# Key norm per token instead of per element: sums of ten columns, spread back by transposes

## The chip, the cores and the metric

The kernel runs on one core of a Trainium2 chip. The metric is device time in microseconds for one execution; the time before is 3225.3 us, the median of three runs from 3222.83 to 3228.34 us.

## What is computed

One layer of a hybrid network over 640 tokens (512 latent, 128 context). Of the input projection's columns, k (1024 wide, 16 heads of 64) goes through the part that the change touches:

```python
kk = heads(k * lp['k_k'])
kk = kk * lax.rsqrt(jnp.maximum(jnp.sum(kk * kk, axis=-1, keepdims=True), 1e-24))
...
kd = heads(k * (1.0 + (a - 1.0) * lp['k_a']))
y, s_fin = _delta_scan(rh, decay, kd, vh, -kk, kk * heads(a), ...)
# in a step: sa = S @ a_t;  S = S * w_t + outer(sa, b_t) + outer(v_t, k_t)
```

The scan meets the normalised key twice, as `a_t = -kk` (it reads the state) and as `b_t = kk * a` (it writes to it), and only as their product. Both norms may therefore stand in `b_t` alone, as one factor 1/sum.

## The kernel before

The work has three stretches. The first, up to about 1090 us, is the input projection: 43 blocks of 128 output columns, each block 16 slices of 128 inputs by two halves of 320 tokens. Every slice takes three `big` products on PE (L190 to L192; high times high, high times low, low times high). The weights come in by DMA as `raw`, ACT rounds them to `hi` (L168) and DVE subtracts to get `lo` (L169); three buffers of each turn over. The second stretch runs the recurrence chunk by chunk beside the output projection, the third is the feed-forward part.

Between the projection's products stands the preparation of the scan. The 16 heads are handled as 8 pairs, one pair on 128 partitions (channels) by 640 tokens. For each pair `take_r`, `take_v` and `take_k` are generators: they run a few instructions, then `yield` a number. A `Mixer` calls them after every second product slice with a budget; a float is charged to the budget, an integer n means "hold for n more slices". The `solve` and `merge` generators of other mixers, and the loads of modulation weights (`pm<-wt,cT`, L903), are laid between as well. The Tile framework's scheduler then sets the final order on every engine.

The key norm is in `take_k`. Before: `nkk` = k times `k_k` on DVE (L565); its square `sqk` on ACT (L567); two PE products with `bones`, a block matrix of ones, give each channel its head's sum, spread over all 64 channels of the head (`pmm`, L519, 128x320 each); DVE clamps them from PSUM into `ssq` (L570), ACT takes the root (L572), DVE inverts it (L576) and multiplies it into `nkk` with a minus sign (L578). What follows for each of two scan directions d: the low-rank products `pwa` (L592, L593), `tanh` (L596), a running sum, `exp`, the read rows `R` (L615 to L621, from `nkk`), the write rows `X` (L632, L636, from `tha` times `nkk`), then PE products of `X` and `R` (`pG`, L651), transposes `pXT` (L669) and `pW` (L683). `pmm` and `pwa` use two PSUM banks, `g0` and `g1` of pool `pk`, one buffer each; `pvt`, `pblk` and the like share two buffers `pt`. At its end `take_k` sums `fs` with `bones` into the same `g0`/`g1` banks, and DVE reads them in `zv` (L698).

Of the kernel before, what the change touches and what calls it, by code (L numbers as in the profile page):

```python
# [10 lines left out]
F32 = mybir.dt.float32  # L11
F32R = mybir.dt.float32r
BF16 = mybir.dt.bfloat16
AF = mybir.ActivationFunctionType
ALU = mybir.AluOpType
# [4 lines left out]
P = 128  # L20
D = 2048
KB = D // P
T = 640
NT = T // P
HALF = T // 2
CH = 64
# [21 lines left out]
NW = 8  # L48
# [27 lines left out]
C_KK = 140  # L76
# [13 lines left out]
def flow_step(ctx: ExitStack, tc, x_prompt, x_sample, state_rwkv, c, c_ctx, w_mod, b_mod,  # L90
# [4 lines left out]
    V, S, G, TE = nc.vector, nc.scalar, nc.gpsimd, nc.tensor  # L95
# [19 lines left out]
    ident = cp.tile([P, P], F32, name="ident")  # L115
    make_identity(nc, ident)
    I2 = cb.tile([P, CH], F32, name="I2")
    for h in range(2):
        s = slice(CH * h, CH * h + CH)
# [7 lines left out]
                         op0=ALU.mult, op1=ALU.add)  # L127
    V.tensor_sub(mask[:, 0:CH], mask[:, CH:P], I2)
    bones = cb.tile([P, P], F32, name="bones")
# [9 lines left out]
    prm = cp.tile([P, NPRM], F32, name="prm")  # L139
# [66 lines left out]
    with ExitStack() as ph:  # L206
# [92 lines left out]
        for t in range(NT):  # L299
            xt = xall[:, t, :]  # L300
            ss = p0b.tile([P, 1], F32, name="ss")
# [5 lines left out]
            for q in range(4):  # L307
                pt = ps0.tile([P, 4, P], F32, tag="pt", name="ptx")
# [31 lines left out]
        for j in range(4):  # L340
# [5 lines left out]
            for kb in range(4 * j, 4 * j + 4):  # L346
                hf = p0b.tile([P, T], F32, name="hf")
# [14 lines left out]
    bk, bp, gs, bz = (hp.enter_context(tc.tile_pool(name=n, bufs=1)) for n in ("bk", "bp", "gs", "bz"))  # L362
# [27 lines left out]

    w0h = bk.tile([P, 32], F32, name="w0h", bufs=1)
    V.tensor_scalar_mul(w0h, prm[:, C_W0:C_W0 + 32], 0.5)
    kah = bk.tile([P, 8], F32, name="kah", bufs=1)
    V.tensor_scalar_mul(kah, prm[:, C_KA:C_KA + 8], 0.5)
    ka1 = bk.tile([P, 8], F32, name="ka1", bufs=1)
# [105 lines left out]
    def both(name):  # L501
        return [pk.tile([P, 512], F32, tag=f"g{h}", name=name) for h in range(2)]
# [10 lines left out]
    def pmm(rhs_list, evac):  # L513
        two = both("pmm")
        for hf in range(2):
            s = slice(HALF * hf, HALF * hf + HALF)
            ps = two[hf][:, 0:HALF]
            for i, (l, r) in enumerate(rhs_list):
                TE.matmul(ps, l, r[:, s], start=(i == 0), stop=(i == len(rhs_list) - 1))  # L519
            evac(ps, s)  # L520
# [29 lines left out]
    def take_k(pr, p):  # L550
# [3 lines left out]
        zk = bk.tile([P, T], F32, tag="zk", name="zk")  # L554
# [7 lines left out]
        S.copy(wh, wl)  # L562
        V.tensor_sub(wr, wl, wh.bitcast(F32))
        nkk = bk.tile([P, T], F32, tag="nkk", name="nkk", bufs=1)
        V.tensor_scalar_mul(nkk, zk, prm[:, C_KK + p:C_KK + p + 1])  # L565
        sq = bk.tile([P, T], F32, tag="t1", name="sqk", bufs=2)
        S.activation(sq, nkk, AF.Square)  # L567
        yield 0.5
        ssq = bp.tile([P, T], F32, tag="t2", name="ssq", bufs=1)
        pmm([(bones, sq)], lambda ps, s: V.tensor_scalar_max(ssq[:, s], ps, 1e-24))  # L570
        yield 1.0
        S.activation(ssq, ssq, AF.Sqrt)  # L572
        yield 0.5
        for hf in range(2):
            s = slice(HALF * hf, HALF * hf + HALF)
            V.reciprocal(ssq[:, s], ssq[:, s])  # L576
            yield 2.0
        V.scalar_tensor_tensor(out=nkk, in0=nkk, scalar=-1.0, in1=ssq, op0=ALU.mult, op1=ALU.mult)  # L578
        fs = bk.tile([P, T], F32, tag="fs", name="fs", bufs=1)
        yield 0.8  # L580
        for d in range(2):
# [4 lines left out]
            tha = bp.tile([P, T], F32, tag="t3", name="tha", bufs=1)  # L586
            for hf in range(2):
                s = slice(HALF * hf, HALF * hf + HALF)
                pwa = both("pwa")
                two = [pwa[h][:, 0:HALF] for h in range(2)]  # L590
# [10 lines left out]
            for lo in (0, HALF):  # L601
                s = slice(lo, lo + HALF)
# [26 lines left out]
            V.tensor_scalar(f, tha, kah[:, p:p + 1], ka1[:, p:p + 1], op0=ALU.mult, op1=ALU.add)  # L629
            V.tensor_mul(f, f, zk)  # L630
            yield 1.2
            V.scalar_tensor_tensor(out=tha, in0=tha, scalar=1.0, in1=nkk, op0=ALU.add, op1=ALU.mult)  # L632
            yield 0.8

            for e in ((0, 1), (1, 0)):
                V.scalar_tensor_tensor(out=rev(X[hsl(e[0]), :, e[1], :]), in0=v3(tha)[hsl(e[0])], scalar=-0.5,  # L636
                                       in1=i3[hsl(e[0])], op0=ALU.mult, op1=ALU.mult)
# [11 lines left out]
            for (c0, c1) in ((0, 4), (4, 8), (8, NCH)):  # L649
                two = [ps.rearrange("p (c t) -> p c t", t=P) for ps in both("pG")]  # L650
# [5 lines left out]
                for h in (1, 0):  # L656
                    s, q, ps = hsl(h), osl(h), two[h]
# [9 lines left out]
            for (c0, c1) in ((0, 8), (8, NCH)):  # L667
                two = [ps.rearrange("p (c t) -> p c t", t=CH) for ps in both("pXT")]
# [3 lines left out]
                for h in range(2):  # L672
                    ps = two[h]
# [4 lines left out]
            two = [ps.rearrange("p (c t) -> p c t", t=CH) for ps in both("pW0")]  # L678
            for c0 in (0, 5):
                ps = two[c0 // 5][:, 0:5, :]  # L680
# [8 lines left out]
            for gq in range(8):  # L689
# [6 lines left out]
                               op0=ALU.mult, op1=ALU.mult)  # L696
# [232 lines left out]
    for p in range(NPAIR):  # L929
        block(P * p, take_r, 2.6, p)  # L930
        block(2 * DA + P * p, take_v, 5.1, p)
        block(DA + P * p, take_k, KCOST, p)
        while g < GORD[p]:
            block(CSH + DA + P * g, take_gv, 12.0, g)
            block(CSH + P * g, take_gu, 5.0, g)
            g += 1
# [36 lines left out]
    pt_ = pbx.enter_context(tc.tile_pool(name="pt_", bufs=2, space=PSUM))  # L973
# [384 lines left out]
    t1, t2 = slice(0, HALF), slice(HALF, T)  # L1358
# [67 lines left out]
    with ExitStack() as ph:  # L1426
        pss = ph.enter_context(tc.tile_pool(name="pss", bufs=1, space=PSUM))
# [5 lines left out]
                        in1=prm[:, C_N2:C_N2 + KB].unsqueeze(2).to_broadcast([P, KB, 2]), op=ALU.mult)  # L1433
        ss = [pss.tile([P, HALF], F32, name=f"ss{hf}") for hf in range(2)]
# [32 lines left out]
        def four_blocks(hf, m, q):  # L1467

            s = slice(HALF * hf, HALF * hf + HALF)
            if q == 0:  # L1470
                pool = pb2 if m % 2 or hf == 0 and m == 4 else pbig
                banks[m] = pool.tile([P, HALF], F32, tag="big", name="big")
            ps = banks[m]
            hi, lo = split(w_out[0, 4 * q * P:(4 * q + 4) * P, m * P:(m + 1) * P], 4,
                           *((wraw, wo) if q or hf or m >= AHEAD else ()))
            for k in range(4):
                kb = 4 * q + k
                TE.matmul(ps, hi[:, k, :], o_hi[kb][:, s], start=(kb == 0), stop=False)  # L1478
                TE.matmul(ps, hi[:, k, :], o_lo[kb][:, s], start=False, stop=False)  # L1479
                TE.matmul(ps, lo[:, k, :], o_hi[kb][:, s], start=False, stop=(kb == 7))  # L1480
            return ps
# [3 lines left out]
        for hf in range(2):  # L1485
            s = slice(HALF * hf, HALF * hf + HALF)
            for m in range(KB):
                if hf or m >= AHEAD:
                    four_blocks(hf, m, 0)
                ps = four_blocks(hf, m, 1)  # L1490
# [591 lines left out]
    for t in (3, 4, 0, 1, 2):  # L2082
        for h in (1, 0):
            out = fin.tile([P, 4, 256], F32, tag=f"out{h}", name="out")
# [3 lines left out]
            else:  # L2088
                V.scalar_tensor_tensor(out=out, in0=src, scalar=rse[:, t:t + 1],
                                       in1=fg[:, 4 * h:4 * h + 4], op0=ALU.mult, op1=ALU.mult)  # L2090
# [31 lines left out]
```

## Time and profile before

| | |
|---|---|
| median of 3 runs | 3225.3 us |
| profiled execution | 3226.49 us |
| its span, first to last instruction | 3224.7 us |
| PE / DVE / ACT / POOL busy over the span | 96% / 72% / 45% / 38% |
| mean granted TensorE clock | 0.990 |

The profile names groups by line, engine and operation, then output tiles `<-` input tiles. A row of a group ends with its busy time, the mean duration of one in ns, and the idle time of the engine just before it with what ended that idle time. `PEld` is the weight load. PE durations are modelled and overlap, so the distance from one start to the next tells the cost of a PE instruction better than its duration.

### The profile page before, as it was taken

To read this page: it belongs to the slowest core of one execution; us is meant where nothing else is said; L and a number is where in the kernel's file an instruction comes from. 1 tells how busy PE (TensorE), PEld (TensorE's weight loads), DVE (VectorE), ACT (ScalarE), POOL (GpSimd) and SP (SyncE) were. 2 spreads that over 40 slices of the span, in tenths; PEclk is the share of its full clock that TensorE was granted. 3 is DMA by queue.
4 is the path that set the end of the run, shared out by engine and by line. 5 is a ranking of instruction groups with operands and counts; after the bars stand their busy time and mean duration, and the time that the engine had idled before them with its cause. 6 is when DMAs were issued, how large, how long until landed. Compare 5 with 4: busy or idle time off the path is not lost.

```text
span 3224.7 us, 72310 instructions
## 1 busy us (share of the span) xinstructions
PE 3097.7 (96%) x28216; PEld 2861.5 (89%) x28216; DVE 2337.3 (72%) x4107; ACT 1460.7 (45%) x3197; POOL 1215.7 (38%) x1065
## 2 busy tenths in 40 slices
PE   6999999999999999999999999999999999999997
PEld 4688778777878888899999999999999999999997
DVE  4547666676666677767877777778788688777778
ACT  3334444444444444346644444444444454444365
POOL 2001121211122023311366556656655645555542
PEclk9999999999999999999999999999999999999999
DMA  9667786777778688564534433343344364553453
GB/s 372 220 197 203 194 215 187 204 205 197 201 197 220 193 273 268 178 197 128 149 112 125 121 117 118 117 128 120 107 130 128 104 197 151 157 157 111 145 167 121
DMA packets 740438, 550.88 MB, mean 171 GB/s; under 512 B 141056, under 2 KB 673504, under 8 KB 731264
## 3 DMA queue, kind: packets, MB, share of 16 engines
q1 hardware_dynamic: 727136, 532.47, 55.5%
q0 software_dynamic: 10624, 13.23, 1.7%
q8 instruction: 222, 3.64, 0.5%
q14 instruction: 120, 0.98, 0.1%
q10 hardware_dynamic: 2336, 0.57, 0.1%
HBM read 437.79 MB, written 110.95 MB: 170 GB/s over the span
## 4 chain that ended last, share of the span: by engine, by line
PE 72%; DVE 10%; DMA 8%; issue 5%; ACT 3%; POOL 2%; SPq 0%; DVEq 0%; POOLq 0%; ACTq 0%
PE P L1640 15%; PE P L1638 15%; PE P L1639 15%; PE big L190 5%; PE big L192 4%; PE big L191 4%; DVE lo L1420 2%; DMA wt<-in_w_mod_dram 2%; PE pm L903 1%; PE pG L651 1%; DMA raw<-in_w_in_dram 1%; PE big L1035 1%; PE big L1479 1%; PE big L1478 1%; PE big L1480 1%
## 5 line engine op out<-in xcount | busy, mean ns | idle before, releaser
L1640 PE MATMUL P<-xo,lo 128*128 128x320 f32 x2352 | 727.9, 310 | 2.2 <-DVE lo L1420 2.1
L1638 PE MATMUL P<-xo,hi 128*128 128x320 f32 x2352 | 727.5, 309 | 0.7 <-ACT hi L1419 0.7
L1639 PE MATMUL P<-xo,hi 128*128 128x320 f32 x2352 | 727.4, 309 | 0.0
L1420 DVE TENSOR_TENSOR lo<-raw,hi 128x512 fp32r<-128x512 f32 x526 | 512.0, 977 | 164.8 <-ACT hi L1419 160.3
L1419 ACT CAST hi<-raw 128x512 fp32r<-128x512 f32 x526 | 327.7, 623 | 487.6 <-PE P L1639 393.5
L190 PE MATMUL big<-h_hi,hi 128*128 128x320 f32 x1376 | 450.4, 327 | 10.1 <-ACT hi L168 6.7
L1640 PEld LDWEIGHTS P<-xo,lo 128*128 128x128 f32 x2352 | 442.1, 188 | 3.2 <-DVE lo L1420 2.9
L1638 PEld LDWEIGHTS P<-xo,hi 128*128 128x128 f32 x2352 | 442.0, 188 | 1.0 <-ACT hi L1419 1.0
L1639 PEld LDWEIGHTS P<-xo,hi 128*128 128x128 f32 x2352 | 442.0, 188 | 0.0
L192 PE MATMUL big<-h_hi,lo 128*128 128x320 f32 x1376 | 433.8, 316 | 0.8 <-DVE lo L169 0.6
L191 PE MATMUL big<-h_lo,hi 128*128 128x320 f32 x1376 | 431.7, 314 | 0.5 <-DVE h_lo L352 0.5
L1548 POOL TENSOR_TENSOR raw<-raw 128x512 f32<-128x512 f32 x252 | 406.6, 1623 | 16.4 <-DVE lo L1420 4.9
L1640 PE MATMUL P<-xd,lo 128*128 128x320 f32 x1232 | 384.9, 312 | 16.3 <-DVE lo L1420 16.3
L1638 PE MATMUL P<-xd,hi 128*128 128x320 f32 x1232 | 383.4, 311 | 1.8 <-ACT hi L1419 1.1
L1639 PE MATMUL P<-xd,hi 128*128 128x320 f32 x1232 | 382.1, 310 | 0.0
L190 PEld LDWEIGHTS big<-h_hi,hi 128*128 128x128 f32 x1376 | 261.9, 190 | 79.0 <-issue 47.8
L169 DVE TENSOR_TENSOR lo<-raw,hi 128x512 fp32r<-128x512 f32 x268 | 183.3, 687 | 195.0 <-ACT hi L168 177.7
L1419 ACT CAST hi<-rawd 128x512 fp32r<-128x512 f32 (+1 forms) x288 | 168.7, 589 | 241.9 <-PE P L1639 201.7
L192 PEld LDWEIGHTS big<-h_hi,lo 128*128 128x128 f32 x1376 | 261.3, 190 | 9.5 <-issue 2.8
L191 PEld LDWEIGHTS big<-h_lo,hi 128*128 128x128 f32 x1376 | 261.8, 190 | 6.0 <-DVE h_lo L352 1.2
L168 ACT CAST hi<-raw 128x512 fp32r<-128x512 f32 x268 | 164.9, 619 | 223.8 <-PE big L191 115.8
L1640 PEld LDWEIGHTS P<-xd,lo 128*128 128x128 f32 x1232 | 232.4, 189 | 22.9 <-DVE lo L1420 22.7
(404 smaller groups left out, 6046.4 us busy)
## 6 DMA issues: line engine op xcount, KB each, us to landing
wt<-in_w_mod_dram SPq DMA_DIRECT2D x96, 1024.0 KB
raw<-in_w_ffn_gate_dram SPq DMA_DIRECT2D x182, 256.0 KB
raw<-in_w_ffn_up_dram SPq DMA_DIRECT2D x182, 256.0 KB
rec<-d_S SPq DMA_DIRECT2D x80, 576.0 KB
raw<-in_w_in_dram SPq DMA_DIRECT2D x172, 256.0 KB
rawd<-in_w_ffn_down_dram SPq DMA_DIRECT2D x128, 256.0 KB
raw<-in_w_out_dram SPq DMA_DIRECT2D x96, 256.0 KB
xd<-d_os SPq DMA_DIRECT2D x66, 320.0 KB
```

The costliest lines, as they stand in the source:

```text
L168: S.copy(hi, raw)
L169: V.tensor_sub(lo, raw, hi.bitcast(F32))
L190: TE.matmul(halves[hf], hi[:, k, :], h_hi[:, kb, s], start=(kb == 0), stop=False)
L191: TE.matmul(halves[hf], hi[:, k, :], h_lo[:, kb, s], start=False, stop=False)
L192: TE.matmul(halves[hf], lo[:, k, :], h_hi[:, kb, s], start=False, stop=(kb == KB - 1))
L651: in_turn([lambda cc=cc, h=h: TE.matmul(two[h][:, cc - c0, :], X[hsl(h), cc].rearrange("p s t -> p (s t)"), R[hsl(h), cc].rearrange("p s t ...
L1419: S.copy(hi[:, 0:nk], raw[:, 0:nk])
L1420: V.tensor_sub(lo[:, 0:nk], raw[:, 0:nk], hi[:, 0:nk].bitcast(F32))
L1548: G.tensor_tensor(out=o[:, 0:nk], in0=p[:, 0:nk], in1=q[:, 0:nk], op=ALU.subtract)
L1638: TE.matmul(ps, hi[:, k, :], xk[:, 0, :], start=f, stop=False)
L1639: TE.matmul(ps, hi[:, k, :], xk[:, 1, :], start=False, stop=False)
L1640: TE.matmul(ps, lo[:, k, :], xk[:, 0, :], start=False, stop=l)
```

## The change

The norm is worked out with tokens on the partitions. `nkk` = minus k times `k_k` is made on ACT, with a column `nkc` prepared once. Five PE products take a 128x128 block of `sqk` as the stationary operand and two columns of `bones` as the moving one, so a token's two head sums lie in two columns (`pss`, 10 columns for 640 tokens, in a `pt` buffer). DVE clamps and inverts these ten columns (`ssk`); ACT repeats each value 64 times (`rnb`, 128x640); after a hold of `NW` = 8 slices five PE transposes put it back to channels by tokens (`pnk`, in `g0`/`g1`), and DVE multiplies it from PSUM with `nkk` into a new tile `nks`. There is no square root: the factor is 1/sum. `R` takes the plain `nkk`; only `tha`, and so `X`, takes `nks`.

```diff
+    nkc = bk.tile([P, 8], F32, name="nkc", bufs=1)
+    V.tensor_scalar_mul(nkc, prm[:, C_KK:C_KK + 8], -1.0)
...
         nkk = bk.tile([P, T], F32, tag="nkk", name="nkk", bufs=1)
-        V.tensor_scalar_mul(nkk, zk, prm[:, C_KK + p:C_KK + p + 1])
+        S.activation(nkk, zk, AF.Copy, scale=nkc[:, p:p + 1])
         sq = bk.tile([P, T], F32, tag="t1", name="sqk", bufs=2)
         S.activation(sq, nkk, AF.Square)
+        yield 0.8
+        ps = pt_.tile([P, 4, P], F32, tag="pt", name="pss")[:, 0, 0:2 * NT].rearrange("p (t h) -> p t h", h=2)
+        for t in range(NT):
+            TE.matmul(ps[:, t, :], sq[:, t * P:(t + 1) * P], bones[:, 0:P:CH], start=True, stop=True)
+        ss = bp.tile([P, NT, 2], F32, name="ssk")
+        V.tensor_scalar_max(ss, ps, 1e-24)
+        V.reciprocal(ss, ss)
+        rb = bk.tile([P, NT, 2, CH], F32, tag="t1", name="rnb", bufs=2)
+        S.copy(rb, ss.unsqueeze(3).to_broadcast([P, NT, 2, CH]))
+        yield NW
+        two = both("pnk")
+        for t in range(NT):
+            TE.transpose(two[t // 3][:, (t % 3) * P:(t % 3 + 1) * P], rb[:, t].rearrange("p h k -> p (h k)"), ident)
         yield 0.5
-        ssq = bp.tile([P, T], F32, tag="t2", name="ssq", bufs=1)
-        pmm([(bones, sq)], lambda ps, s: V.tensor_scalar_max(ssq[:, s], ps, 1e-24))
-        yield 1.0
-        S.activation(ssq, ssq, AF.Sqrt)
-        yield 0.5
-        for hf in range(2):
-            s = slice(HALF * hf, HALF * hf + HALF)
-            V.reciprocal(ssq[:, s], ssq[:, s])
-            yield 2.0
-        V.scalar_tensor_tensor(out=nkk, in0=nkk, scalar=-1.0, in1=ssq, op0=ALU.mult, op1=ALU.mult)
+        nks = bk.tile([P, T], F32, tag="nks", name="nks", bufs=1)
+        for t0, t1 in ((0, 3), (3, NT)):
+            V.tensor_mul(nks[:, t0 * P:t1 * P], nkk[:, t0 * P:t1 * P], two[t0 // 3][:, 0:(t1 - t0) * P])
...
-            V.scalar_tensor_tensor(out=tha, in0=tha, scalar=1.0, in1=nkk, op0=ALU.add, op1=ALU.mult)
+            V.scalar_tensor_tensor(out=tha, in0=tha, scalar=1.0, in1=nks, op0=ALU.add, op1=ALU.mult)
```

The new lines move the scheduler's order within the projection stretch only; on PE the last 14891 instructions stand as before. Three places follow.

On PE, at the third pair's norm, before:

```order
L192 MATMUL big<-h_hi,lo 128x320
L519 MATMUL pmm<-sqk,bones 128x320 x2
L190 MATMUL big<-h_hi,hi 128x320
L191 MATMUL big<-h_lo,hi 128x320
L192 MATMUL big<-h_hi,lo 128x320
```

and at the same pair now (`pm_3491` is a modulation product that happens to stand there):

```order
L573 MATMUL pss<-bones,sqk 128x2 x5
L191 MATMUL big<-h_lo,hi 128x320
L192 MATMUL big<-h_hi,lo 128x320
L190 MATMUL big<-h_hi,hi 128x320
L191 MATMUL big<-h_lo,hi 128x320
L192 MATMUL big<-h_hi,lo 128x320
L911 MATMUL pm_3491<-wt,cT 2x512
L582 MATMUL pnk<-ident,rnb 128x128 x5
```

Two products have become ten instructions in two groups, with five `big` products between them. In the eight pairs 9, 24, 5, 24, 9, 24, 24 and 12 `big` products stand between the groups.

On ACT, at the second pair's norm, before:

```order
L567 ACTIVATE sqk<-nkk 128x640
L168 CAST hi<-raw 128x512
L572 ACT_TABLE_LOAD
L572 ACTIVATE ssq<-ssq 128x640
L168 CAST hi<-raw 128x512
L596 ACT_TABLE_LOAD
L596 ACTIVATE sg<-pwa,w0h 128x320
```

and now:

```order
L567 ACTIVATE nkk<-zk,nkc 128x640
L569 ACTIVATE sqk<-nkk 128x640
L627 COPY R<-nkk 128x10
L168 CAST hi<-raw 128x512
L578 COPY rnb<-ssk 128x640
L168 CAST hi<-raw 128x512
L604 ACTIVATE sg<-pwa,w0h 128x320
```

Both table loads are gone (in the whole program 19 became 3), and the spread `rnb` stands behind a weight cast. That is so in pairs 2, 4, 6, 7 and 8.

On DVE, at the second pair's norm, before:

```order
L565 TENSOR_SCALAR nkk<-zk,prm 128x640
L169 TENSOR_TENSOR lo<-raw,hi 128x512
L570 TENSOR_SCALAR ssq<-pmm 128x320 x2
L576 RECIPROCAL ssq<-ssq 128x320 x2
L169 TENSOR_TENSOR lo<-raw,hi 128x512
L578 SCALAR_TENSOR_TENSOR nkk<-nkk,ssq 128x640
```

and now:

```order
L575 TENSOR_SCALAR ssk<-pss 128x10
L576 RECIPROCAL ssk<-ssk 128x10
L169 TENSOR_TENSOR lo<-raw,hi 128x512
L586 TENSOR_TENSOR nks<-nkk,pnk 128x384
L586 TENSOR_TENSOR nks<-nkk,pnk 128x256
L169 TENSOR_TENSOR lo<-raw,hi 128x512
```

The wide clamp and inversion have become narrow; the multiplication now stands in DVE's queue until PE's transposes are done.

## The prediction

> **What bounds the kernel now.** First the page's head and its table of busy times, then the busy times cut into the projection stretch that holds the whole change (139 to 1090 us), then that stretch's groups and PE's waits, then the timeline for the price of single pieces.
>
> ```profile
> span 3224.7 us, 72310 instructions
> PE 3097.7 (96%) x28216; PEld 2861.5 (89%) x28216; DVE 2337.3 (72%) x4107; ACT 1460.7 (45%) x3197; POOL 1215.7 (38%) x1065
> ```
>
> The columns of the next row are the stretch and its length, then PE, PEld, DVE, ACT and POOL with their instructions, granted clock, DMA share and GB/s.
>
> ```profile
> 139.00:1090.00 951.00, 911.38 (x10787) 768.94 (x10788) 625.82 (x1243) 436.53 (x940) 159.59 (x259) 0.99 0.72 196
> ```
>
> PE is busy 911.4 of 951 us, DVE 625.8 (66%), ACT 436.5 (46%). So PE sets the end of the stretch; all that it waits for comes to 951 - 911.4 = 39.6 us. Work taken from DVE or ACT pays only through these waits. The next rows are PE's waits there: total us, times, longest.
>
> ```profile
> PE pG L651 <- DVE X L636: 5.1, 8, 1.6
> PE pm L903 <- DMA wt<-in_w_mod_dram: 4.6, 5, 2.4
> PE pG L651 <- DVE GA L661: 3.5, 4, 2.1
> PE big L190 <- ACT hi L168: 3.2, 5, 1.0
> PE pXT L669 <- DVE GA L661: 2.8, 6, 0.7
> PE pmm L519 <- DVE zv L698: 2.8, 3, 2.0
> PE pXT L669 <- ACT XT L675: 2.7, 5, 0.7
> PE pG L651 <- DVE X L640: 1.5, 2, 1.1
> ```
>
> No row is large. One belongs to the norm itself: `pmm`, which waits for the PSUM banks that DVE still reads in `zv`.
>
> **Off PE.** The groups of the norm (count, busy us, mean ns, idle time ahead):
>
> ```profile
> L576 DVE RECIPROCAL ssq<-ssq 128x320 f32<-128x320 f32 x16 | 33.7, 2132 | 4.0 <-ACT ssq L572 4.0
> L660 DVE TENSOR_TENSOR GR<-pG,mask 128x256 f32<-128x256 f32 x64 | 27.0, 422 | 20.1 <-PE pG L651 10.0 <-DMA d_S<-GR 8.9
> L572 ACT ACT_TABLE_LOAD x8 | 10.3, 1283 | 0.1
> L596 ACT ACT_TABLE_LOAD x8 | 10.3, 1283 | 0.1
> L698 DVE TENSOR_TENSOR zv<-pmm,zv 128x320 f32<-128x320 f32 x16 | 7.7, 481 | 0.3 <-PE pmm L519 0.3
> L570 DVE TENSOR_SCALAR ssq<-pmm 128x320 f32<-128x320 f32 x16 | 7.3, 485 | 2.3 <-PE pmm L519 2.1
> L578 DVE SCALAR_TENSOR_TENSOR nkk<-nkk,ssq 128x640 f32<-128x640 f32 x8 | 6.5, 814 | 0.0
> L572 ACT ACTIVATE ssq<-ssq 128x640 f32<-128x640 f32 x8 | 5.9, 740 | 11.5 <-DVE ssq L570 11.5
> L565 DVE TENSOR_SCALAR nkk<-zk,prm 128x640 f32<-128x640 f32 x8 | 4.6, 572 | 0.1
> L747 DVE TENSOR_SCALAR gva<-gva 128x5 f32<-128x5 f32 x7 | 1.2, 172 | 0.1
> ```
>
> DVE loses per pair 0.57 + 2 x 0.485 + 2 x 2.13 + 0.81 = 6.6 us. It gains a clamp and an inversion of ten columns, about 0.2 us each (estimate: the 128x5 row's 172 ns; ten columns of the inversion at 2132/320 = 6.7 ns are 67 ns more at most), and the product out of PSUM, 384 and 256 columns: 256 cost 422 ns and 320 cost 481 ns in the rows, so 0.55 + 0.42 = 0.97 us. Net -5.2 us a pair, -42 us in all. ACT loses 2 x 1.283 + 0.74 = 3.3 us a pair and gains `nkk` and `rnb`, each about the 0.74 us of another 128x640 row; net -1.8, or -14 us in all. Together that is 56 of 1062 us, or 5%.
>
> **On PE.** Now the timeline (start, us, engine, line): the norm's two products, a group of four transposes, and a group of `pW` products on 64x64 blocks.
>
> ```profile
> 193.72 0.30 PE L192 MATMUL big<-h_hi,lo 128*128 128x320 f32 x1
> 193.93 1.34 PE L519 MATMUL pmm<-sqk,bones 128*128 128x320 f32 x4
> 194.87 0.55 PE L190 MATMUL big<-h_hi,hi 128*128 128x320 f32 x1
> 195.25 0.31 PE L191 MATMUL big<-h_lo,hi 128*128 128x320 f32 x1
> 195.40 0.31 PE L192 MATMUL big<-h_hi,lo 128*128 128x320 f32 x1
> ...
> 182.32 0.31 PE L192 MATMUL big<-h_hi,lo 128*128 128x320 f32 x1
> 182.46 0.60 PE L544 MATMUL pvt<-ident,zv 128*128 128x128 f32 x4
> 182.82 0.39 PE L190 MATMUL big<-h_hi,hi 128*128 128x320 f32 x1
> 183.05 0.31 PE L191 MATMUL big<-h_lo,hi 128*128 128x320 f32 x1
> ...
> 588.17 0.31 PE L191 MATMUL big<-h_lo,hi 128*128 128x320 f32 x1
> 588.41 0.80 PE L683 MATMUL pW<-Z,GA 64*64 64x64 f32 x20
> 589.14 0.42 PE L192 MATMUL big<-h_hi,lo 128*128 128x320 f32 x1
> 589.39 0.31 PE L190 MATMUL big<-h_hi,hi 128*128 128x320 f32 x1
> ```
>
> `big` products follow each other at 0.147 us (195.25 to 195.40). From 193.72 to 195.25 go 1.53 us; less two spacings of 0.147 that is 1.24 us for the old products. Four transposes: 182.32 to 183.05 less the same is 0.44 us, 0.11 each, so the five new ones cost 0.55 us. Twenty `pW` records: 588.17 to 589.39 less two spacings is 0.93 us, 0.046 each.
>
> The five `pss` products have no row like them: a full 128x128 f32 stationary operand and only two moving columns. An f32 product makes two records here (16 `pmm` products of the norm, 32 records), so there are ten. The lower bound is the `pW` row, 0.046 each, 0.46 us; the upper is the 0.11 us of a transpose, which loads the same weights and streams 128 columns, 1.1 us. I take 0.1 us, near the upper row, because it has the same weights. Then the new PE work is 1.0 + 0.55 = 1.55 us against 1.24: +0.31 a pair, **+2.5 us** for eight; by the bounds (0.46 and 1.1) -1.8 to +3.3 us.
>
> The Trainium skill has two rules for this piece, and they part. "TensorE: Matmul & The Clock Gate", section "Back-to-back issue gap", gives up to 64 moving columns a floor of about 25 ns, which would make ten records 0.25 us and this term -3.5 us. Its section "LDWEIGHTS (loading the stationary operand)" prices a load by its columns, P/1.2 ns, 107 ns for 128, whatever streams through, which makes it 1.07 us and this term +3.0 us: that speaks against making the wide operand the stationary one. No row here separates load and stream.
>
> The order takes switches away. A `pW` group, on part of the array, has 588.17 to 588.41 = 0.24 us ahead of it and 589.14 to 589.39 = 0.25 us behind its first `big`, where 0.147 is normal: 0.2 us a switch. Counting over the stretch's whole order, switches from `big` to groups on part of the array fall by 15 (`pXT` 40 to 29, `pG`, `pT` and `pM` by 8 together; `pblk` and `pm` rise by 4): **-3.0 us**, bounds 0 and -3.
>
> **Waits.** `pss` no longer needs the banks that `zv` holds: the `pmm` row goes, **-2.8 us**. If `pnk` meets `zv` in its place it stays; the hold makes that unlikely.
>
> The new wait is `pnk` for `rnb`: clamp 0.2, inversion 0.2 to 0.24, copy 0.74, about 1.2 us after the last `pss`. On PE 9, 24, 5, 24, 9, 24, 24 and 12 `big` products stand between, 1.3, 3.5, 0.7, 3.5, 1.3, 3.5, 3.5 and 1.8 us. Only the third pair falls short, by 0.5 us at most. But ACT and DVE work in order, and a cast stands ahead of `rnb` in five pairs; I take **+1.0 us** in all, bounds 0 and the slow rival below.
>
> The rest is the looser DVE. `X` waits behind the inversions in the first of two directions: half of 5.1 + 1.5, -3.3 us. The other waits on DVE and ACT, some 20 us of the 39.6, shrink by perhaps a tenth where the load shrinks by 5%: -2.0 us. Together **-5.3 us**; bounds 0 and -20 (half of all that PE waits).
>
> Sum: 2.5 - 3.0 - 2.8 + 1.0 - 5.3 = **-7.6 us**. The profiled execution, 3226.49 us (span 3224.7 and 1.8 around it), goes to 3218.9; it lies 1.2 us over the median, so by the median 3225.3 - 7.6 = 3217.7, forecast **3218**. Its own range is 3212 to 3222.
>
> **Rivals.** *The norm's DVE block was what the pair waited for.* The reciprocal holds DVE for 4.3 us a pair, and everything behind it, masks, `X` and `lo`, is late at once. Then half of PE's waits go in place of the 5.3: -20 and the PE terms -2.3, 3203. For it: five of the eight rows above are waits on DVE. Against it: those five are 15.7 us together, half of it on masks and `zv`, which do not follow the norm.
>
> *Nothing changes.* If DMA paces the stretch (0.72 busy, and PE waits 4.6 us for `wt`), what PE saves it waits for elsewhere: 3225. Against it: 4.6 us is all that is seen.
>
> *Slower: the transposes wait for ACT.*
>
> ```profile
> L168 ACT CAST hi<-raw 128x512 fp32r<-128x512 f32 x161 | 99.0, 619 | 129.1 <-PE big L191 112.2 <-DMA raw<-in_w_in_dram 14.4 <-issue 1.8
> ...
> ACT hi L168 <- PE big L191: 112.2, 71, 4.5
> ```
>
> A cast waits for PE to leave a weight buffer, 1.6 us on average when it waits, 4.5 at the longest. If it stands ahead of `rnb` and is released by a `big` shortly before the transposes, PE then waits for cast and copy, 0.62 + 0.74 = 1.36 us, and DVE holds its `lo` behind `nks`. It decides from a wait of 3.5 - 1.2 = 2.3 us on. In eight pairs that is +10.9; with the 5.3 lost and the other terms (2.5 - 3.0 - 2.8) it makes +7.6: 3233. For it: a cast is there in five of eight pairs. Against it: 2.3 us is above the mean.
>
> **How the numbers follow.** Forecast 0.55, large gain 0.18, nothing 0.12, slower 0.15. The range takes the large gain's centre and goes up to near the slow one, 3203 to 3230. A measurement tells about 0.2%, 6.5 us, from no change, so faster is below 3218.8. A little over half of the forecast lies there and all of the large gain: 0.3 + 0.18 = 0.48. Slower is 0.15, with 0.01 from the rest; within 0.2% is what is left, 0.36.
>
> **What would show it.** In the profile after, the stretch should have DVE near 584 us and ACT near 422; ten `pss` records about 0.1 us apart; no `pmm<-sqk` wait; rows `pnk <- ACT rnb` of at most 1 us or so in total; `X` and `GA` waits down by a third. `pss` at 0.05 apart gives 4 us more. Rows of `pnk` waiting in most pairs, with `hi` ahead of `rnb` late, would make the prediction wrong upwards; PE waits of 20 us in place of 39.6, downwards.

## The result and the profile after

| | before | after |
|---|---|---|
| median, runs | 3226.82 us (3222.83 to 3235.99, 4 runs) | 3258.62 us (3250.72 to 3262.37, 4 runs) |
| ratio | | 1.0094, 95% interval 1.0078 to 1.0110 |
| profiled execution, span | 3226.49, 3224.7 us | 3255.12, 3253.3 us |
| mean granted clock | 0.990 | 0.987 |

The change makes the kernel slower by 0.94%, about 30 us; 7.6 us less was predicted. These are the page's span and busy times after, and then the projection stretch, which now ends near 1114 us instead of 1089 (columns as in the prediction).

```profile
span 3253.3 us, 72457 instructions
PE 3115.5 (96%) x28304; PEld 2873.6 (88%) x28304; DVE 2292.9 (70%) x4092; ACT 1445.8 (44%) x3189; POOL 1219.0 (37%) x1065
```

```profile
139.00:1114.00 975.00, 927.36 (x10862) 781.99 (x10861) 584.84 (x1224) 421.95 (x927) 158.52 (x259) 0.98 0.70 191
```

Read DVE and ACT first. DVE has 584.8 us in the stretch and ACT 421.9, where 584 and 422 were forecast: what was taken off these engines is gone. But PE now needs 975 us for the stretch instead of 951. It is busy 927.4 instead of 911.4, and it stands still for 975 - 927.4 = 47.6 us instead of 39.6. The rest of the program takes 3 us more; 25 of the 29 us of span are in this stretch.

PE's waits in the stretch (total us, times, longest):

```profile
PE pm L911 <- DMA wt<-in_w_mod_dram: 7.7, 9, 1.5
PE big L190 <- ACT hi L168: 4.9, 6, 1.3
PE pG L659 <- DVE X L644: 4.2, 5, 1.7
PE pblk L851 <- issue: 3.7, 2, 3.0
PE pblk L851 <- DMA TB<-d: 3.7, 4, 1.9
PE ptm L176 <- issue: 3.0, 2, 2.6
PE pG L659 <- DVE GA L669: 2.8, 7, 0.7
PE pmm L521 <- ACT Z L693: 2.5, 3, 2.0
PE pG L659 <- DVE X L648: 2.3, 3, 1.1
```

No row is large, as before, but they are other rows. The wait for `zv` is gone. In its place stand waits of `pblk` and `ptm` (10.4 us in three rows, each of which stood at 0.7 us or less), and more for `wt`, `hi` and `Z` (2.5 us; before 0.9). The two `X` rows are 6.5 us, and a third of 1.0 us is new; before they were 6.6. `pnk` for `rnb` is not among them at all. Added up by what ended them, PE's waits on DVE and ACT fell from 33.1 to 29.0 us, and 2.8 of that is the row for `zv`. The waits on a DMA, or with no releaser named, rose from 6.5 to 18.5 us.

Now the new PE work itself, in PE's timeline of the first pair (start, us, line):

```profile
192.91 0.30 PE L190 MATMUL big<-h_hi,hi 128*128 128x320 f32 x1
193.22 1.28 PE L573 MATMUL pss<-bones,sqk 128*128 128x2 f32 x10
194.35 0.39 PE L191 MATMUL big<-h_lo,hi 128*128 128x320 f32 x1
194.58 0.31 PE L192 MATMUL big<-h_hi,lo 128*128 128x320 f32 x1
...
195.61 0.31 PE L190 MATMUL big<-h_hi,hi 128*128 128x320 f32 x1
195.76 0.77 PE L582 MATMUL pnk<-ident,rnb 128*128 128x128 f32 x5
196.29 0.39 PE L191 MATMUL big<-h_lo,hi 128*128 128x320 f32 x1
196.52 0.31 PE L192 MATMUL big<-h_hi,lo 128*128 128x320 f32 x1
```

The ten records take 193.22 to 194.35 = 1.13 us, 0.113 each, though each streams two columns. Summed from start to start over all eight pairs, `pss` is 8.9 us and `pnk` 4.9 where the two old products were 8.8: +5.0 us.

Last, what a wait costs here. The timeline of PE around one of the new waits, and then four stretches of 3.4 us around it (PE's busy time is the first number after the length, the granted clock the third from the end):

```profile
753.27 0.50 PE L851 MATMUL pblk<-TB,M 32*32 32x32 f32 x35
756.76 0.32 PE L851 MATMUL pblk<-TB,M 32*32 32x32 f32 x15 [2.99 <-issue]
757.01 1.01 PE L911 MATMUL pm<-wt,cT 128*2 128x512 f32 x4
```

```profile
750.20:753.60 3.40, 3.40 (x150) 3.17 (x137) 0.06 (x1) 0.76 (x2) 0.00 (x0) 1.00 1.05 307
753.60:757.00 3.40, 0.41 (x31) 0.28 (x20) 3.02 (x7) 1.19 (x3) 0.00 (x0) 1.00 0.21 62
757.00:760.40 3.40, 3.40 (x58) 1.64 (x48) 0.91 (x2) 0.08 (x1) 0.00 (x0) 0.51 0.28 46
760.40:763.80 3.40, 3.40 (x33) 2.81 (x33) 0.18 (x1) 1.03 (x3) 0.00 (x0) 0.98 0.83 286
```

PE waits 3 us in the second stretch and is given half the clock in the third, with work at hand: 3.4 us at 0.5 lose another 1.7. The trace's clock record has 13.6 us of half clock in this stretch of the program before and 34 us after, which is 10.2 us of clock lost on top. So the 25 us come apart as +5.0 of new PE work, +8.0 of standing still and +10.2 of half clock; some 2 us are left that I did not trace further.

Not every half-clock stretch follows a wait. One of 6.8 us begins at 610.1 us. In the 3.4 us ahead of it PE was busy throughout, but 1.03 us of that went to the ten `pss` records of the fifth pair, and 0.9 to products on 32x32 blocks:

```profile
606.70:610.10 3.40, 3.40 (x61) 2.97 (x60) 1.79 (x9) 0.92 (x2) 0.37 (x1) 1.00 0.91 263
610.10:613.50 3.40, 3.40 (x48) 2.96 (x49) 1.08 (x4) 1.08 (x4) 0.00 (x0) 0.53 1.00 304
```

### The profile page after: what moved, and what is told of

It reads as the page before. It is cut to its first block, busy times and chain, and to the rows that moved or that the text cites. A ratio compares the mean times of both kernels' runs of the same rounds, so it can differ in the third digit from the quotient of the medians.

```text
span 3253.3 us, 72457 instructions
## 1 busy us (share of the span) xinstructions
PE 3115.5 (96%) x28304; PEld 2873.6 (88%) x28304; DVE 2292.9 (70%) x4092; ACT 1445.8 (44%) x3189; POOL 1219.0 (37%) x1065
## 4 chain that ended last, share of the span: by engine, by line
PE 58%; DVE 6%; DMA 6%; issue 4%; POOL 3%; ACT 2%; SPq 0%; POOLq 0%; DVEq 0%; ACTq 0%
PE P L1648 14%; PE P L1646 14%; PE P L1647 14%; PE big L190 2%; PE big L192 1%; DVE lo L1428 1%; PE big L191 1%; DMA wt<-in_w_mod_dram 1%; DMA rawd<-in_w_ffn_down_dram 1%; PE big L1488 1%; PE big L1486 1%; PE big L1487 1%; PE big L1043 1%; POOL rawd L1556 1%; PE big L1045 1%
## 5 line engine op out<-in xcount | busy, mean ns | idle before, releaser
L1428 DVE TENSOR_TENSOR lo<-raw,hi 128x512 fp32r<-128x512 f32 x526 | 502.7, 959 | 173.7 <-ACT hi L1427 169.7
L169 DVE TENSOR_TENSOR lo<-raw,hi 128x512 fp32r<-128x512 f32 x268 | 184.4, 692 | 205.1 <-ACT hi L168 203.4
```

Of the source, the lines that this page charges most:

```text
L169: V.tensor_sub(lo, raw, hi.bitcast(F32))
L1428: V.tensor_sub(lo[:, 0:nk], raw[:, 0:nk], hi[:, 0:nk].bitcast(F32))
```

## The experiments

Each ratio is against runs of the kernel before on the same chip, with its 95% interval. The question is why PE stands still more, with two engines relieved.

**The pace alone.** The old operations with the changed kernel's yields and hold.

```diff
         S.activation(sq, nkk, AF.Square)
-        yield 0.5
+        yield 0.8
...
-        yield 1.0
         S.activation(ssq, ssq, AF.Sqrt)
-        yield 0.5
+        yield NW
...
             V.reciprocal(ssq[:, s], ssq[:, s])
-            yield 2.0
```

> The norm's instructions as before, but its yields as in the change (0.8, a hold of 8 slices, then 0.8 instead of 0.5, 1.0, 0.5, 2.0, 2.0, 0.8). Theory A (the shorter budget and the hold shift the pair's later work, solve and merge against the big products; the new order costs waits): most of the change's loss is here, +18 to +30 us over before. Theory B (the new PE instructions and their place cost it): within 5 us of before.

Measured: 3238.24 us, ratio 1.0053 (1.0040 to 1.0065). With not one operation changed, half of the loss is there, and one row holds it:

```profile
PE pblk L842 <- DMA TB<-d: 22.3, 3, 7.6
```

PE reaches the block products of `merge` before the tile that they read has come back by DMA. Its other waits are shorter, so PE stands still for 44.5 us in the stretch where it was 39.6; the clock lost there rises by 6.9 us.

**The operations alone.** The changed operations with the old yields (no hold, 0.5, 1.5 and 4.0 in its place).

```diff
-        yield 0.8
+        yield 0.5
         ps = pt_.tile([P, 4, P], F32, tag="pt", name="pss")[:, 0, 0:2 * NT].rearrange("p (t h) -> p t h", h=2)
...
-        yield NW
+        yield 1.0
+        yield 0.5
         two = both("pnk")
...
-        yield 0.5
+        yield 2.0
+        yield 2.0
```

> The changed kernel with the yields of before (sum 6.8 and no hold, the transposes 1.5 after the sums). Theory A: the loss goes, before +0 to +10 us. Theory B: the loss stays, +25 to +35 us.

Measured: 3260.19 us, 1.0120 (1.0105 to 1.0136). No wait for `TB` is left, and yet all of the loss is there, in `X`, `hi`, `zv` and `Z`. So neither the pace alone nor the wait for `TB` makes the loss.

**The sums twice.** The ten `pss` records are issued a second time.

```diff
         for t in range(NT):
             TE.matmul(ps[:, t, :], sq[:, t * P:(t + 1) * P], bones[:, 0:P:CH], start=True, stop=True)
+        for t in range(NT):
+            TE.matmul(ps[:, t, :], sq[:, t * P:(t + 1) * P], bones[:, 0:P:CH], start=True, stop=True)
```

> The changed kernel with the five token sums issued twice for each pair (40 more products, the same result). The trace of the change has ten pss records in about 1.05 us, so PE gets 8.4 us more. Theory B (PE bound, its work adds straight): +8 to +10 us over the changed kernel, 3266 to 3270. Theory A does not forbid that, but if the time moves by far more or far less than 8 us, the place in the order counts more than the work.

Measured: 3272.49 us, 1.0157 (1.0143 to 1.0172). Against the change's 1.0094 that is about +20 us for 9.1 us more of PE work. The rest is clock, and here no wait is ahead of it. In five of the eight pairs half clock begins right behind the twenty records, though PE was busy all through the 3.4 us before. The second pair, with the columns as above:

```profile
305.10:308.50 3.40, 3.40 (x30) 3.03 (x33) 0.17 (x1) 1.46 (x3) 0.00 (x0) 1.00 1.21 156
308.50:311.90 3.40, 3.40 (x17) 2.35 (x10) 0.77 (x2) 0.72 (x1) 0.00 (x0) 0.54 0.37 101
```

In these five windows `pss` takes 1.75 to 2.33 us from start to start; in the other windows that hold `pss`, with 1.58 us at most, the clock stays. The five stretches of half clock are 20.5 us long and lose 10.2. So a PE that is busy with products of two moving columns can be given half the clock like one that stands still.

**The merge held longer.** `HOLD` 68 becomes 80 in the changed kernel, so that `TB` has time to land.

```diff
-HOLD = 68
+HOLD = 80
```

> The changed kernel with the merge held 80 slices after its loads are issued instead of 68. The trace of the change has PE waiting 3.7 us for the merge's loads (TB) and 3.7 us more ahead of the same products with no releaser named, with half-clock windows behind them. Theory A (the shorter pace brings the merge ahead of its loads): these waits go, 8 to 14 us below the changed kernel. Theory B (the new PE instructions cost it, through their time and the clock): within 4 us of the changed kernel.

Measured: 3274.48 us, 1.0157 (1.0136 to 1.0179). The waits for `TB` went, others grew, and the time with them: the theory that the merge's loads are the loss falls. The same edit in the kernel **before**:

> The kernel before with the merge held 80 slices instead of 68. Its trace shows no wait for TB, so a later merge has nothing to win: 0 to +5 us. If any new order costs 10 us or more here too, what the change lost is the fit of the constants to the old order rather than its own work.

Measured: 3257.77 us, 1.0109 (1.0088 to 1.0130), +35 us with no change of work at all. In its profiled execution, the longest of the six, 16 us of the loss lie in this stretch and 26 behind it.

**Wider sums.** 96 moving columns instead of two in each token sum.

```diff
-            TE.matmul(ps[:, t, :], sq[:, t * P:(t + 1) * P], bones[:, 0:P:CH], start=True, stop=True)
+            TE.matmul(ps[:, t], sq[:, t * P:(t + 1) * P], bones[:, 16:112], start=True, stop=True)
```

> The changed kernel with 96 moving columns (48 of each head) in each token sum instead of 2; DVE still reads two of them. Theory L (a sum's time is its weight load): pss records stay about 0.1 us apart, at most +1 us of PE time. Theory G (the clock gate goes to half after a 3.4 us window in which PE streams little, and two-column products stream next to nothing): the half-clock windows that come right behind pss go, and the time falls by 3 to 8 us. If a record's time is its stream, PE gets 2 us more and nothing falls.

Measured: 3248.84 us, 1.0082 (1.0058 to 1.0106), no different from the change within the intervals. In its one profiled execution, the longest of the six, half clock begins right behind `pss` in no pair, as theory G had it; but it comes elsewhere, and the stretch loses 25.6 us of clock (17.1 in the change). The timeline of its first pair:

```profile
194.13 1.35 PE L573 MATMUL pss<-bones,sqk 128*128 128x96 f32 x10
195.27 0.39 PE L191 MATMUL big<-h_lo,hi 128*128 128x320 f32 x1
```

Ten records of 96 columns take 1.14 us, ten of two columns 1.13. So the price does not lie in what streams; the stationary operand, 128x128 in both, is what is left to pay for.

**The sums in the old banks.** `pss` goes to `g0` instead of a `pt` buffer.

```diff
-        ps = pt_.tile([P, 4, P], F32, tag="pt", name="pss")[:, 0, 0:2 * NT].rearrange("p (t h) -> p t h", h=2)
+        ps = both("pss")[0][:, 0:2 * NT].rearrange("p (t h) -> p t h", h=2)
```

> The changed kernel with the token sums in the banks g0/g1 that the old sums used, instead of the shared pt buffers. If the wait for a pt buffer (late pss in three pairs) matters, 5 us or more less; if not, within 4 us. The wait for zv that the old sums had may come back, +3 us.

Measured: 3251.38 us, 1.0084 (1.0064 to 1.0104). It differs from the change by no more than the intervals, so the buffer is not the cause.

**A light norm at the old operations**: neither root nor table loads, inversions of ten columns, a constant in place of the norm.

```diff
-        pmm([(bones, sq)], lambda ps, s: V.tensor_scalar_max(ssq[:, s], ps, 1e-24))
+        pmm([(bones, sq)], lambda ps, s: V.tensor_scalar(ssq[:, s], ps, 1e-24, 0.015, op0=ALU.max, op1=ALU.min))
+        rj = bp.tile([P, 2, 10], F32, name="rj")
         yield 1.0
-        S.activation(ssq, ssq, AF.Sqrt)
...
-            V.reciprocal(ssq[:, s], ssq[:, s])
+            V.reciprocal(rj[:, hf], ssq[:, s][:, 0:10])
```

> The kernel before, yields and PE products as they are, with the norm's other work taken away: no root and no table loads on ACT (-3.3 us a pair), inversions of 10 columns instead of 320 on DVE (-3.9 us a pair). The norm itself is left out (a clamped constant stands for it). The merges stay at their places against the big products. Theory R (a looser DVE and ACT shorten PE's waits, as the prediction counted): 5 to 20 us below before. Theory N (nothing that PE waits for hangs on that load): within 4 us.

Measured: 3239.18 us, 1.0053 (1.0040 to 1.0066). DVE and ACT have less to do, PE the same, and it is 16 us slower, which neither theory had.

**The PE work alone.** The kernel before issues the ten sums and five transposes as well, and nothing uses them.

```diff
+        ps = pt_.tile([P, 4, P], F32, tag="pt", name="pss")
+        for t in range(NT):
+            TE.matmul(ps[:, 0, 2 * t:2 * t + 2], sq[:, t * P:(t + 1) * P], bones[:, 0:P:CH], start=True, stop=True)
+        for t in range(NT):
+            TE.transpose(ps[:, 1 + t % 3, :], sq[:, t * P:(t + 1) * P], ident)
         yield 1.0
         S.activation(ssq, ssq, AF.Sqrt)
```

> The kernel before with the change's new PE work added and nothing removed: ten pss records and five transposes for each pair, their results unused; the merges stay in place. The new work takes 1.6 us a pair by the trace of the change, 13 us in all. Straight addition: +13 us. Theory G (two-column products count as idle PE, and a half-clock window follows): +18 to +30 us, with half-clock windows right behind pss.

Measured: 3236.95 us, 1.0045 (1.0030 to 1.0060): +13 us for 12.9 us of PE work (8.6 and 4.3, from start to start). Half clock begins right behind `pss` in no pair, with ten of its records at a time, and the mean granted clock of the executions is that of before (0.9897 against 0.9901). So PE work costs its length here, though this edit lays the order anew as well and the match may be partly luck. The net +5 of the change is a sixth of the loss.

**A neutral shift.** In the kernel before, the yields 0.5 (ahead of the sums) and 1.0 (behind them) change places.

```diff
-        yield 0.5
+        yield 1.0
         ssq = bp.tile([P, T], F32, tag="t2", name="ssq", bufs=1)
         pmm([(bones, sq)], lambda ps, s: V.tensor_scalar_max(ssq[:, s], ps, 1e-24))
-        yield 1.0
+        yield 0.5
```

> The kernel before with two of its yields exchanged (1.0 then 0.5 for 0.5 then 1.0): no work differs, the order differs at about 4% of PE's places, the merges begin at the same slices but for two. If any shift of the tuned order costs, +5 to +20 us; if it is the merge against its loads that counts, within 4 us.

Measured: 3228.99 us, 1.0021 (1.0008 to 1.0033), 7 us for two numbers that do no work.

**No root.** The old spread sums, inverted without a root, used in the write rows alone: the change's algebra with the old PE work and yields.

```diff
-        S.activation(ssq, ssq, AF.Sqrt)
...
-        V.scalar_tensor_tensor(out=nkk, in0=nkk, scalar=-1.0, in1=ssq, op0=ALU.mult, op1=ALU.mult)
+        nks = bk.tile([P, T], F32, tag="nks", name="nks", bufs=1)
+        V.tensor_mul(nks, nkk, ssq)
```

> The kernel before with the factor 1/sum in the write rows alone (as in the change), but the sums still spread by bones and inverted at full width: no root and no table loads, the same PE work and yields. Theory R: 2 to 8 us below before. Theory N: within 4 us.

Measured: 3252.65 us, 1.0098 (1.0080 to 1.0117): as slow as the change, with none of its PE work.

Up to here each edit had also made the scheduler lay PE's instructions anew: at 1926 of the 22,982 places the light norm has another instruction than before, without the root 1892. The next runs hold the order. All PE instructions are chained, each behind the one that stands ahead of it in the kernel whose order is wanted; that adds no semaphore.

```diff
+    for a, b in zip(order, order[1:]):
+        tc.add_manual_dep(pe[b], pe[a].name, ...NoSync..., reason="order")
```

**The light norm and the missing root at the old order.**

> The kernel before with the light norm (no square root, no table loads, 10-column inversions, the norm itself left out for a constant), as in the run of the light norm, but TensorE now issues its 22,982 products and transposes in exactly the order of the kernel before; the other engines keep the order that the scheduler gives them. Theory O (the loss is the new order of TensorE's instructions): back to the time before or a little under it, 3217 to 3229 us. Rival W (the lighter norm itself upsets the stretch, wherever TensorE's instructions stand): it stays at the light norm's 3239 us, 3235 to 3243.

> The kernel before without the square root on the spread norm (its inverse is used in the writing rows alone, as in the run without the root), with TensorE's order held to that of the kernel before. Theory O: 3220 to 3232 us, the time before within 0.2 per cent, since TensorE's work and order are those of before. Rival W: it stays at the 3252 us of the run without the root, 3246 to 3258.

Measured: 3222.48 us, 0.9995 (0.9984 to 1.0005), and 3225.57 us, 1.0001 (0.9989 to 1.0013). Both losses, 16 and 29 us, are gone, with no work altered, only the order. It is not PE's alone: the scheduler lays the other engines around it. Leaving the norm's own instructions aside, some 120 of DVE's 4027 and some 90 of ACT's 2951 stood out of the old sequence in the program of the light norm; with PE's order held it is some 40 and 15. Much of both losses was clock. By the mean granted clock of all executions, times the span, the light norm had lost 9.5 us more than before and the kernel without the root 23; at the old order they lose 3 and 2 us less. The stretch with the light norm at the old order:

```profile
139.00:1090.00 951.00, 913.36 (x10795) 771.01 (x10792) 595.50 (x1245) 412.67 (x918) 159.28 (x259) 0.99 0.70 196
```

DVE is 30 us and ACT 24 us lighter than before, and PE does as much in 951 us as it did (911.4). For these two kernels the order, PE's and what comes with it, is shown to be the whole loss; and at a fixed order the relief is worth -1.6 us, with an interval from -5.2 to +1.6.

**The change at the old order, and the old operations at the new one.** The same chain. The first has the yields of before and the sums in `g0`; the five token sums stand where the first of the old products stood and the transposes 9 to 13 instructions behind. In the second the old products stand where the token sums stand in the change.

> The changed operations, the token sums in the g0 bank, TensorE's order held to that of the kernel before: the ten-record sums stand where the two 320-column products stood, the five transposes 9 to 13 instructions behind them, and everything else in the order of before. Theory O: the time before plus the straight price of TensorE's added work, 13 to 14 us for sums and transposes less 8.8 us for the old products, so 3227 + 5 = 3232 us, 3225 to 3237. Rival W (the new operations or their new waits cost the time by themselves): 3249 to 3261 us, as the change.

> The mirror image: the operations of before, with TensorE's order held to that of the changed kernel (the two 320-column products stand where the ten-record sums stand there, the transposes are gone). Theory O: the time of the change less the straight 5 us, 3253 us, 3245 to 3258. Rival W: the time before, or that of the old operations at the new pace at most, 3225 to 3240 us.

Measured: the change at the old order 3248.76 us, 1.0087 (1.0063 to 1.0111); the old operations at the order of the change 3263.42 us, 1.0120 (1.0100 to 1.0139). The first came out at the edge of its rival W (3249 to 3261), the second beyond what theory O said (3245 to 3258). So the new order by itself costs the old operations 39 us: PE waits 13.8 us for `X` there, in three rows, where it was 6.6. But the old order does not save the change, as the pure order theory said. This run holds PE's order alone, and one place shows what that leaves open. First ACT and DVE there in the kernel before:

```profile
272.54 0.85 ACT L685 COPY Z<-pW 64x320 f32<-64x320 f32 x2 [1.15 <-PE pW L683]
278.81 0.74 ACT L711 ACTIVATE gq<-gq 128x640 f32<-128x640 f32 x1 [5.42 <-DVE gq L709]
275.05 0.19 DVE L802 COPY mx<-mix 80x30 f32<-80x30 f32 x1 [3.83 <-DMA mix<-dd]
```

Then the same in the change at the old order, and PE's wait for it:

```profile
279.64 0.74 ACT L721 ACTIVATE gq<-gq 128x640 f32<-128x640 f32 x1 [6.52 <-DVE gq L719]
280.40 0.85 ACT L695 COPY Z<-pW 64x320 f32<-64x320 f32 x2
277.31 0.19 DVE L812 COPY mx<-mix 80x30 f32<-80x30 f32 x1 [2.69 <-DMA mix<-dd]
```

```profile
PE pmm L521 <- ACT Z L695: 6.8, 3, 5.8
```

In both kernels DVE stands at a copy for the merge whose data has not landed, with `gq` queued behind it, and ACT waits for `gq`. Before, that cost PE nothing: ACT had copied `Z` ahead of the wait. Now the scheduler has put `Z` behind `gq`, and PE waits for `Z`, 5.8 us at the longest.

**All three engines at the old order.** VectorE and ScalarE are chained in the same way; their new instructions stand where the old ones of the norm stood.

```diff
-    for a, b in zip(order, order[1:]):
+    for own, order in ((pe, pe_order), (dve, dve_order), (act, act_order)):
+        for a, b in zip(order, order[1:]):
```

> The change at the order of before on TensorE, as in the run that held TensorE alone, and now VectorE and ScalarE held to the order of before as well: the new maximum and inversion of the ten columns stand where VectorE read the first half of the old sums, the copy that spreads the factor stands where ScalarE took the square root, and the two multiplications out of PSUM stand where the factor was multiplied on before. Theory O, extended to the other engines (the run with TensorE alone held kept 25 us because ScalarE and VectorE were laid anew, with one wait of 5.8 us for Z): the time before plus the straight 5 us, 3225 to 3238 us, and no wait for Z above 2 us. Rival W (the new operations cost the rest by their own waits at any order): it stays at 3243 to 3256 us.

Measured: 3255.11 us, 1.0098 (1.0079 to 1.0118). The order theory fails here too. In the profiled execution (3271.47 us, the longest of its six) one wait is new; in the run that held PE alone it was 0.4 us:

```profile
PE pwa L602 <- DVE nks L588: 9.2, 6, 5.2
```

`pnk` keeps the two banks `g0` and `g1` until DVE has multiplied out of them; the old sums left them as soon as DVE had clamped them. So the banks are held for longer by the place of two DVE instructions; the next run differs in that place alone.

> As the run that held the order of all three engines, but VectorE's two multiplications out of PSUM stand where it took the first of the two 320-column inversions, about 5 us earlier in its queue, so that the two banks of the spread factor come free earlier. Theory N (at the old order the change pays because its spread factor keeps the two banks that the products pwa need next, 9.2 us in six waits, and each long wait brings a stretch at half clock): the wait of pwa for nks falls under 2 us and the time to 3229 to 3243 us. Rival W (the rest is spread over other waits, so nothing comes back): 3246 to 3260 us.

In VectorE's order, by what stood there before:

```diff
 ssk clamp and inversion     (where the first half was clamped)
+nks multiplications         (where the first half was inverted)
...
-nks multiplications         (where nkk was multiplied)
```

Measured: 3243.39 us, 1.0060 (1.0047 to 1.0074), 12 us back (4 to 20 by the two intervals), and the wait for `nks` is gone; `pnk` now waits 3.3 us for `rnb`, in two waits. In the profiled execution (3238.3 us, the shortest of its five) the projection stretch ends 4.9 us later than before: 4.0 us of new PE work (`pss` 8.8 and `pnk` 4.0 for 8.8) and 3.4 of lost clock, less 2.1 of standing still. The other 6.9 us lie behind the stretch. There PE's wait for `bv`, before and in this run, and this run's clock around it:

```profile
PE pmm L1266 <- DVE bv L1267: 1.1, 1, 1.1
```

```profile
PE pmm L1276 <- DVE bv L1277: 2.5, 1, 2.5
```

```profile
1255.00:1258.40 3.40, 1.62 (x26) 1.36 (x28) 2.20 (x6) 1.69 (x8) 0.00 (x0) 1.00 0.49 169
1258.40:1261.80 3.40, 3.01 (x58) 2.59 (x58) 2.83 (x10) 1.67 (x8) 2.43 (x5) 0.51 0.76 227
1261.80:1268.60 6.80, 6.80 (x87) 5.55 (x83) 4.08 (x15) 2.44 (x13) 6.23 (x8) 0.50 0.59 188
```

A wait that is 1.4 us longer is followed by 10.2 us at half clock, 5.1 us lost; the kernel before has no half clock at that place. It has some at others: over all that lies behind the stretch half clock is 13.7 us before and 20.5 here, so 3.4 of the 6.9 us are clock.

## Why the prediction was wrong

By its own steps:

- *DVE -42, ACT -14 us.* Right: over the span DVE fell from 2337.3 to 2292.9 and ACT from 1460.7 to 1445.8.
- *PE work +2.5 us.* The mechanism was right, the size was not: +5.0. In the first pair the ten records took 1.13 us and not 1.0, and with the entry from a `big` product 1.38 (192.91 to 194.58 less two spacings), the transposes 0.62 and not 0.55. The Trainium skill's "TensorE: Matmul & The Clock Gate", section "LDWEIGHTS (loading the stationary operand)", prices a load by the columns of the stationary operand alone, 107 ns for 128: the 113 ns, and 96 columns at the price of two, agree with it. The prediction set the floor of 25 ns in the Trainium skill's section "Back-to-back issue gap" against this. That section says itself that its isolated gap counts no weight load at small sizes, so the two rules do not part, as the prediction read them; the 113 ns are four times the floor.
- *Fewer switches -3.0 us.* Not seen. From start to start and without their waits, the groups on part of the array took as much as before: `pXT` -0.7 and `pG` -1.1 us, but `pT` +1.0 and `pblk` +2.0.
- *No wait for `zv`, -2.8 us; `pnk` for `rnb`, +1.0.* Both rows did as forecast, the second with less. But other rows grew by more (`pblk`, `ptm`, `wt`).
- *Looser DVE and ACT, -5.3 us.* This step failed. The waits on DVE and ACT fell by 4.1 us, and 2.8 of these are the `zv` row that was counted already, so 1.3 us are left for it. `X`, which was to lose half, waits as long as it did, and the masks `GA` 4.9 us for 6.3. At a fixed order a lighter DVE and ACT are worth nothing that could be measured.
- *What the sum left out.* It counted the moved instructions only as fewer switches, as if the waits of the old order would stay where they are and shrink. This, with the clock, is what turned the sign: waits on a DMA, or with no releaser named, grew by 12.0 us. The order is made anew with every edit of the norm, and a new order makes its own waits: 16 and 29 us in two kernels, shown by giving them the old order back, and 39 us for the old operations at the order of the change. Nor was there a term for the clock, which takes 10 of the 25 us in the stretch.

The slow rival had the sign and not the mechanism: in the change `pnk` never waited for a cast. The rival "nothing changes" had half of its reason right: what PE no longer waited for on DVE and ACT it did wait for elsewhere, a good part of it on DMAs. But its condition, that DMA paces the stretch, is not seen: the DMA share fell from 0.72 to 0.70. The large gain fell with the step on a looser DVE and ACT.

How much of the 30 us is order and how much the operations cannot be put in two numbers, since they do not add: the new order with the old operations costs 39, the new operations at the old order 17 to 30, both together 30. Shown are the 5 us of PE work, that freeing the two banks earlier gave back some 12, and that relief pays nothing measurable at a fixed order. The 17 us that are left at the old order with the banks freed early are 4 of PE work and some 12 of clock: the granted clock averages 0.9864 over the five executions of that run and 0.9901 over the nine of before. Which waits lower it was followed in one execution only, and why the operations of the change bring them at the old order stays open; the queues that issue the DMAs were held in no run. None of the versions is faster than the kernel before.

## What to carry to other kernels

Where one engine is 96% busy and its order is fixed ahead, count only work on that engine; relief elsewhere is worth what its waits on them measurably shrink by, not what those engines save. An edit that makes a scheduler lay that engine's instructions anew is a change of its own, which can cost several times the edit: hold the old order and measure once more before judging the operations. Read the granted clock of every execution too: in most of the slower versions here two fifths to three quarters of the loss stood there. And when a result stays in a PSUM bank until another engine reads it, price the bank's next user as well.

## What was not expected of the hardware

- The granted clock went to 0.5 for stretches of 3.4 us or a few of them, often behind 3.4 us in which PE had little to do: after 0.41 us of PE busy in 3.4 (a wait of 3.0 us), and after 1.62 in 3.4 (a wait of 2.5 us), while the same wait at 1.1 us cost nothing of the kind. Counted over the traces of all 19 kernels, from 139 us on, in windows of 3.4 us laid by the clock record: each of the 90 windows at full clock with PE busy for less than 1.5 us was followed by half clock; of the 15454 with 3.0 us or more, six were. Between the two both happened. The Trainium skill's "TensorE: Matmul & The Clock Gate", section "What's actually happening", has half clock after an idle window of about 3.4 us: the length agrees; these windows were not wholly idle.
- All six of those busy windows hold `pss` records: five of them most or all of a pair's twenty, in the run with the sums twice, and one a pair's ten, in the change. Products of two moving columns keep PE busy in the profile and can still cost the clock.
- A product of two moving columns costs as much as one of 96: 0.113 and 0.114 us a record in the first pair, with a 128x128 f32 stationary operand.
